# Weight sums and activation differences of the second MLP product: from GpSimd to VectorE

## The chip, the cores and the metric

The kernel runs on one core of a Trainium2 chip. The metric is the device time of one execution in microseconds (us), the median of several. Besides TensorE (matrix products; PE in the profile, and PEld for its loads of the stationary operand) the core has VectorE (DVE), ScalarE (ACT), GpSimd (POOL), and SyncE (SP), whose queue starts the transfers from and to memory. Each engine takes its instructions strictly in the order of its own queue.

## The reference

One layer on 512 positions of width 2048 in float32. A mixing part (RMSNorm, a combined projection, stick-breaking attention, a spatial gating unit, gates, an output projection) gives `x = x + out`. It is untouched here. The part that matters is the MLP behind it:

```python
h2 = rms_norm(x, g_ff[l])
x = x + jnp.square(jax.nn.relu(h2 @ w_ff1[l])) @ w_ff2[l]     # w_ff1: 2048 x 8192, w_ff2: 8192 x 2048
```

## The kernel before

**Two halves of every operand.** TensorE is used with a 32-bit type of reduced precision (float32r), so every operand is split into a high half and a low half that together hold the float32 value. One product is three matmuls: high by high (line 68), and the two mixed ones (lines 69 and 70), in `mm3`. ScalarE makes the high half of a weight tile (`w_hi`, lines 90 and 103), then VectorE the low half (`w_lo = raw - w_hi`, lines 92 and 104). A low half can only start when its high half is done, and the matmul of line 69 or 70 that uses it waits for it. The pairs of halves of a weight tile rotate through three places, so a new high half waits until TensorE is through with the tile three before it.

**The MLP loop.** It runs over 16 blocks f of 512 hidden units (`chunks`). In each, `hidden` makes the first product of block f+1 in two parts p of 256 units: 4 weight tiles of 128x1024 by 24 matmuls, 96 in all; then `relu` on VectorE (line 603) and its square on ScalarE (line 604). `strassen` makes the second product of block f, twice (g = 0 and 1, 1024 output columns each). The order on TensorE is: first part of `hidden`, `strassen` g = 0, second part of `hidden`, `strassen` g = 1, so one f has two halves of 96 + 84 = 180 matmuls each.

**Strassen's scheme.** A 2x2 block product takes 7 multiplications instead of 8. Their names in the code, in TensorE's order, are y11, y21, m7, m6, y22, m4 and m5. Each has 12 matmuls (2 position tiles t, 2 tiles k, 3 of `mm3`). On the weight side they take quarters of the matrix or sums of quarters: `plus` (line 165) makes four sums of 128x1024 elements, for m7, m6, y22 and m5, the first only after the low half of y11 has been made from the same buffer. On the activation side `factors` makes four differences of 128x256 elements for each of the two tiles of block f+1 (lines 615 to 618: the `m` tiles), and then splits seven factors (`ys`, 128x256). `factors` for block f+1 falls into the time of `strassen` g = 1 of block f. Every finished product is added to the result tiles by VectorE (line 643, `x`; 16 additions of 128x512 per `strassen`), and these additions also free the accumulators in PSUM that later products need.

**What sets the order.** The tile framework's scheduler sets each engine's queue at build time, from the program's order and its own estimate of durations; nothing is reordered at run time. In the last block (f = 15) there is no `hidden` any more, so the last three `strassen` (g = 1 of block 14, and both of block 15) follow each other directly.

Of the kernel before, what the change touches and what calls it, by code (L numbers as in the profile page):

```python
# [12 lines left out]
ALU = mybir.AluOpType  # L13
# [20 lines left out]
def tile_hybrid_layer(ctx: ExitStack, tc: tile.TileContext, x, g_mix, w_in, g_q, g_k, ln_g, ln_b,  # L34
# [4 lines left out]
    nc = tc.nc  # L39
# [10 lines left out]
    def slot(name, dt=F32, pool=slots):  # L50
        return pool.tile([P, 512], dt, name=name, tag="slot")
# [14 lines left out]
    def mm3(o, lh, rh, start, stop, **kw):  # L66

        nc.tensor.matmul(o, lhsT=lh[0], rhs=rh[0], start=start, stop=False, **kw)  # L68
        nc.tensor.matmul(o, lhsT=lh[0], rhs=rh[1], start=False, stop=False, **kw)  # L69
        nc.tensor.matmul(o, lhsT=lh[1], rhs=rh[0], start=False, stop=stop, **kw)  # L70
# [24 lines left out]
    def split(src, name, scale=None, pool=slots):  # L95

        hi, lo = slot(name + "_hi", F32R, pool), slot(name + "_lo", F32R, pool)
        split_to(hi, lo, src, scale)
        return hi, lo

    def split_to(hi, lo, src, scale=None):
        if scale is None:
            nc.scalar.copy(out=hi, in_=src)  # L103
            nc.vector.tensor_tensor(out=lo, in0=src, in1=f32(hi), op=ALU.subtract)  # L104
        else:
            nc.scalar.activation(out=hi, in_=src, func=AF.Copy, scale=scale)
            nc.vector.scalar_tensor_tensor(out=lo, in0=src, scalar=scale, in1=f32(hi),
                                           op0=ALU.mult, op1=ALU.subtract)
# [31 lines left out]
    def strassen(wap, r0, c0, lhs, evac):  # L140

        KH = 2

        def piece(name):
            return wpool.tile([P, KH, W], F32R, name=name, tag="w_piece", bufs=6)

        def whole(name):
            return state["whole"].tile([P, KH, W], F32, name=name, tag="whole")

        def quarter(h, c):
            raw = whole("w_raw")
            state["load"] = nc.sync.dma_start(
                out=raw, in_=wap[r0:r0 + 2 * KH * P, c0 + c * W:c0 + (c + 1) * W]
                .rearrange("(k h p) c -> h p k c", p=P, h=2)[h])
            return raw

        w11, w12, w21, w22 = quarter(0, 0), quarter(1, 0), quarter(0, 1), quarter(1, 1)
        sc = whole("w_sum")

        def plus(o, a, b):
            nc.gpsimd.tensor_tensor(out=o, in0=a, in1=b, op=ALU.add)  # L165


        made = {"m7": lambda: plus(w11, w11, w21), "m6": lambda: plus(sc, w11, w22),
                "y22": lambda: plus(w12, sc, w12), "m5": lambda: plus(w21, w21, w22)}
        take = {"y11": w11, "y21": w12, "m7": w11, "m6": sc, "y22": w12, "m4": w22, "m5": w21}  # L170
        banks = {}
        for name, b, first, last in (("y11", 0, True, False), ("y21", 1, True, True),
                                     ("m7", 2, True, False), ("m6", 0, False, False),
                                     ("y22", 1, True, True), ("m4", 2, False, True),
                                     ("m5", 0, False, True)):
            if name in made:
                made[name]()
            hi, lo = piece("w_hi"), piece("w_lo")
            split_to(hi, lo, take[name])
            if first:  # L180
                banks[b] = [(aux if b == 1 else acc)("q") for _ in range(2)]
            for t in range(2):
                o = banks[b][t]
                for k in range(KH):
                    y = [part[:, t * P:(t + 1) * P] for part in lhs(k, name)]
                    mm3(o, y, (hi[:, k, :], lo[:, k, :]), first and k == 0, k == KH - 1,
                        skip_group_check=True)
                evac(name, t, o)
# [210 lines left out]
    for half in range(2):  # L399
# [4 lines left out]
                 lambda tb, o, v=v: v.append(split(o, "v", rstd[:, tb:tb + 1])), "v")  # L404
# [205 lines left out]
    def factors(act):  # L610

        y11, y12, y21, y22 = act[0][:, :HS], act[0][:, HS:], act[1][:, :HS], act[1][:, HS:]
        ta, tb = slot("m"), slot("m")
        m7, m6, m4, m5 = ta[:, :HS], ta[:, HS:], tb[:, :HS], tb[:, HS:]
        nc.gpsimd.tensor_tensor(out=m7, in0=y12, in1=y22, op=ALU.subtract)
        nc.gpsimd.tensor_tensor(out=m6, in0=m7, in1=y11, op=ALU.subtract)
        nc.gpsimd.tensor_tensor(out=m4, in0=y21, in1=m6, op=ALU.add)
        nc.gpsimd.tensor_tensor(out=m5, in0=y11, in1=y12, op=ALU.subtract)
        y = {}
        for name, src in (("y11", y11), ("y21", y21), ("m7", m7), ("m6", m6), ("y22", y22),  # L620
                          ("m4", m4), ("m5", m5)):
            t = slot("ys", F32R)
            y[name] = (t[:, :HS], t[:, HS:])
            split_to(*y[name], src)
        return y
# [6 lines left out]
    for f in range(chunks):  # L632
        ys = [factors(act) for act in ahead]
        ahead = []
        for g in range(2):

            if f < chunks - 1:
                ahead.append(hidden(f + 1, g))

            def evac_y(name, t, o):  # L640
                for half, c, op in takes[name]:
                    a = x2[2 * half + t, 2 * g + c]
                    nc.vector.tensor_tensor(out=a, in0=a, in1=o, op=op)  # L643
                    if f == chunks - 1 and (name, half, c) in (("m4", 0, 1), ("y21", 0, 0),
                                                              ("m5", 1, 1), ("m5", 1, 0)):
                        tb, j = 2 * half + t, 2 * g + c
                        nc.sync.dma_start(out=out[tb * P:(tb + 1) * P, j * W:(j + 1) * W], in_=a)

            strassen(w_ff2[0], f * PAIRS * 2 * P, g * 2 * W, lambda k, name: ys[k][name], evac_y)
# [25 lines left out]
```

## Time and profile before

| | us |
|---|---|
| time, median of 3 runs (2574.0 to 2575.1) | 2575.06 |
| time of the profiled execution | 2574.17 |
| its span, first to last instruction | 2572.5 |
| busy: TensorE / VectorE / ScalarE / GpSimd | 2532.1 / 1438.7 / 852.9 / 589.0 |
| start of the first addition of a second product (line 643) | 1286.5 |

The MLP's second product lies in the second half of the span. Matmuls overlap each other: one of 512 columns is shown with 0.39 us, but the next one starts 0.227 us after it. So the distance between starts is what counts for TensorE, and the same is true, to a smaller degree, for VectorE.

### The profile page before, as it was taken

What the parts mean: (1) busy time and instruction counts of PE and PEld (TensorE: products, weight loads), DVE (VectorE), ACT (ScalarE), POOL (GpSimd) and SP (SyncE); (2) the same over time, 40 slices, a digit from 0 to 9 for tenths busy, and PEclk for the clock granted to TensorE, in tenths of its full rate; (3) what the DMA queues carried; (4) which work ended last, traced back from release to release, by engine and by line L of the source; (5) the groups of instructions that cost most, each with busy time, mean ns of one, the idle gap of its engine ahead of it and who ended that gap; (6) DMA issues with size and microseconds to landing.
All of it is one profiled execution on the core that took longest, in us unless ns stands there. A gap on an engine that the chain in (4) does not pass through costs nothing.

```text
span 2572.5 us, 28610 instructions
## 1 busy us (share of the span) xinstructions
PE 2532.1 (98%) x11306; PEld 2082.1 (81%) x11306; DVE 1438.7 (56%) x1806; ACT 852.9 (33%) x1172; POOL 589.0 (23%) x379
## 2 busy tenths in 40 slices
PE   8999999999999999999999999999999999999998
PEld 7888888888888888888878777887778777877786
DVE  4555563333335333333475767667666767576759
ACT  5333342222223222223333333333332334233333
POOL 0211110000211000100223242414342333324244
PEclk9999999999999999999999999999999999999999
DMA  5332323333332333434233323233323333332323
GB/s 172 90 91 74 90 64 99 93 97 98 115 115 78 99 101 93 129 107 133 88 110 95 115 87 111 89 115 97 101 90 107 102 95 99 98 115 82 114 68 121
DMA packets 169574, 259.83 MB, mean 101 GB/s; under 512 B 8368, under 2 KB 77024, under 8 KB 169440
## 3 DMA queue, kind: packets, MB, share of 16 engines
q1 hardware_dynamic: 169440, 258.01, 32.7%
q8 instruction: 89, 1.46, 0.2%
q14 instruction: 45, 0.37, 0.0%
HBM read 253.78 MB, written 4.19 MB: 100 GB/s over the span
## 4 chain that ended last, share of the span: by engine, by line
PE 87%; DVE 10%; issue 1%; ACT 1%; DMA 0%; POOL 0%; SPq 0%; DVEq 0%; ACTq 0%; POOLq 0%
PE f L69 9%; PE f L68 9%; PE f L70 9%; PE q L69 6%; PE q L70 6%; PE q L68 6%; DVE w_lo L104 4%; DVE ys L104 3%; DVE x L643 3%; PE xo L70 2%; PE xo L69 2%; PE xo L68 2%; PE gb L68 2%; PE gb L70 2%; PE gb L69 2%; PE ga L68 2%
## 5 line engine op out<-in xcount | busy, mean ns | idle before, releaser
L92 DVE TENSOR_TENSOR w_lo<-w_raw,w_hi 128x1024 fp32r<-128x1024 f32 x336 | 414.2, 1233 | 686.5 <-ACT w_hi L90 677.7
L90 ACT CAST w_hi<-w_raw 128x1024 fp32r<-128x1024 f32 x336 | 353.7, 1053 | 988.8 <-PE q L69 190.0
L104 DVE TENSOR_TENSOR w_lo<-w_raw,w_hi 128x1024 fp32r<-128x1024 f32 x192 | 281.9, 1469 | 255.8 <-ACT w_hi L103 255.8
L68 PE MATMUL f<-h2T_hi,w_hi 128*128 128x512 f32 x1024 | 398.6, 389 | 0.0
L69 PE MATMUL f<-h2T_lo,w_hi 128*128 128x512 f32 x1024 | 398.5, 389 | 0.0
L70 PE MATMUL f<-h2T_hi,w_lo 128*128 128x512 f32 x1024 | 397.9, 391 | 0.0
L69 PE MATMUL q<-w_lo,ys 128*128 128x512 f32 x896 | 352.8, 394 | 26.4 <-DVE w_lo L104 26.3
L165 POOL TENSOR_TENSOR w_raw<-w_raw 128x1024 f32<-128x1024 f32 x64 | 183.1, 2862 | 820.0 <-DVE w_lo L104 820.0
L70 PE MATMUL q<-w_hi,ys 128*128 128x512 f32 x896 | 349.0, 389 | 0.0
L643 DVE TENSOR_TENSOR x<-x,q 128x512 f32<-128x512 f32 x512 | 331.0, 676 | 2.3 <-PE q L70 0.6
L103 ACT CAST w_hi<-w_raw 128x1024 fp32r<-128x1024 f32 x192 | 201.8, 1053 | 391.2 <-PE f L69 290.3
L68 PE MATMUL q<-w_hi,ys 128*128 128x512 f32 x896 | 324.0, 391 | 1.5 <-DVE x L643 1.2
L69 PEld LDWEIGHTS q<-w_lo,ys 128*128 128x128 f32 x896 | 168.1, 188 | 74.1 <-DVE w_lo L104 40.0
L70 PEld LDWEIGHTS f<-h2T_hi,w_lo 128*128 128x128 f32 x1024 | 192.2, 188 | 44.2 <-DVE w_lo L92 4.6
L69 PEld LDWEIGHTS f<-h2T_lo,w_hi 128*128 128x128 f32 x1024 | 192.2, 188 | 40.1
L68 PEld LDWEIGHTS f<-h2T_hi,w_hi 128*128 128x128 f32 x1024 | 192.3, 188 | 39.4
L68 PEld LDWEIGHTS q<-w_hi,ys 128*128 128x128 f32 x896 | 168.1, 188 | 40.3 <-issue 3.5
L70 PEld LDWEIGHTS q<-w_hi,ys 128*128 128x128 f32 x896 | 168.3, 188 | 33.8
L68 PE MATMUL gb<-hT_hi,w_hi 128*128 128x512 f32 x256 | 100.3, 392 | 0.2 <-DVE gb L413 0.2
L68 PE MATMUL xo<-w_hi,mT_hi 128*128 128x512 f32 x256 | 100.5, 393 | 0.0
L68 PE MATMUL ga<-hT_hi,w_hi 128*128 128x512 f32 x256 | 100.4, 392 | 0.0
L69 PE MATMUL ga<-hT_lo,w_hi 128*128 128x512 f32 x256 | 100.0, 391 | 0.0
(199 smaller groups left out, 3919.4 us busy)
## 6 DMA issues: line engine op xcount, KB each, us to landing
w_raw<-in_w_ff_dram SPq DMA_DIRECT2D x256, 512.0 KB, 3.7
w_raw<-in_w_in_dram SPq DMA_DIRECT2D x144, 512.0 KB, 3.7
w_raw<-in_w_out_dram SPq DMA_DIRECT2D x32, 512.0 KB, 3.7
w_raw<-in_w_oa_dram SPq DMA_DIRECT2D x16, 512.0 KB, 3.7
w_raw<-in_w_ob_dram SPq DMA_DIRECT2D x16, 512.0 KB, 3.6
x<-in_x_dram SPq DMA_DIRECT2D x16, 256.0 KB, 5.3
out_dram<-x SPq DMA_DIRECT2D x16, 256.0 KB, 2.2
xq<-in_x_dram SPq DMA_DIRECT2D x12, 256.0 KB, 6.4
```

Of the source, the lines that this page charges most:

```text
L68: nc.tensor.matmul(o, lhsT=lh[0], rhs=rh[0], start=start, stop=False, **kw)
L69: nc.tensor.matmul(o, lhsT=lh[0], rhs=rh[1], start=False, stop=False, **kw)
L70: nc.tensor.matmul(o, lhsT=lh[1], rhs=rh[0], start=False, stop=stop, **kw)
L90: nc.scalar.copy(out=hi, in_=raw)
L92: nc.vector.tensor_tensor(out=lo, in0=raw, in1=f32(hi), op=ALU.subtract)
L103: nc.scalar.copy(out=hi, in_=src)
L104: nc.vector.tensor_tensor(out=lo, in0=src, in1=f32(hi), op=ALU.subtract)
L165: nc.gpsimd.tensor_tensor(out=o, in0=a, in1=b, op=ALU.add)
L643: nc.vector.tensor_tensor(out=a, in0=a, in1=o, op=op)
```

## The change

In `strassen` the four weight sums, and in `factors` the four differences, are issued to VectorE instead of GpSimd. Nothing else is written differently. These are 32 times 4 sums of 128x1024 and 32 times 4 differences of 128x256.

```diff
         def plus(o, a, b):
-            nc.gpsimd.tensor_tensor(out=o, in0=a, in1=b, op=ALU.add)
+            nc.vector.tensor_tensor(out=o, in0=a, in1=b, op=ALU.add)
...
-        nc.gpsimd.tensor_tensor(out=m7, in0=y12, in1=y22, op=ALU.subtract)
-        nc.gpsimd.tensor_tensor(out=m6, in0=m7, in1=y11, op=ALU.subtract)
-        nc.gpsimd.tensor_tensor(out=m4, in0=y21, in1=m6, op=ALU.add)
-        nc.gpsimd.tensor_tensor(out=m5, in0=y11, in1=y12, op=ALU.subtract)
+        nc.vector.tensor_tensor(out=m7, in0=y12, in1=y22, op=ALU.subtract)
+        nc.vector.tensor_tensor(out=m6, in0=m7, in1=y11, op=ALU.subtract)
+        nc.vector.tensor_tensor(out=m4, in0=y21, in1=m6, op=ALU.add)
+        nc.vector.tensor_tensor(out=m5, in0=y11, in1=y12, op=ALU.subtract)
```

The scheduler puts the moved instructions into VectorE's queue, so its order is new from the first `factors` on. The first place is the end of a second part of `hidden` and the begin of `strassen` g = 1. VectorE's queue before, from the low half of the last `hidden` tiles (L92) over those of y11 and y21 (L104 x2) to that of m6 (from `w_sum`):

```order
L92 TENSOR_TENSOR w_lo<-w_raw,w_hi 128x1024 x2
L104 TENSOR_TENSOR w_lo<-w_raw,w_hi 128x1024 x2
L603 SCALAR_TENSOR_TENSOR relu<-f_9228,rstd_b 128x512
L603 SCALAR_TENSOR_TENSOR relu<-f_9229,rstd_b 128x512
L104 TENSOR_TENSOR w_lo<-w_raw,w_hi 128x1024
L643 TENSOR_TENSOR x_7982<-x_7982,q 128x512
L643 TENSOR_TENSOR x_7984<-x_7984,q 128x512
L104 TENSOR_TENSOR w_lo<-w_sum,w_hi 128x1024
```

The four sums now stand ahead of the two `relu`. Three follow the low half of y11, one that of y21:

```order
L104 TENSOR_TENSOR w_lo<-w_raw,w_hi 128x1024
L165 TENSOR_TENSOR w_raw<-w_raw 128x1024
L165 TENSOR_TENSOR w_sum<-w_raw 128x1024
L165 TENSOR_TENSOR w_raw<-w_raw 128x1024
L104 TENSOR_TENSOR w_lo<-w_raw,w_hi 128x1024
L165 TENSOR_TENSOR w_raw<-w_sum,w_raw 128x1024
L603 SCALAR_TENSOR_TENSOR relu<-f_9228,rstd_b 128x512
L603 SCALAR_TENSOR_TENSOR relu<-f_9229,rstd_b 128x512
```

Behind the second `relu` the low half of m7 and two additions are now mixed with four differences, up to the low half of m6:

```order
L615 TENSOR_TENSOR m<-relu 128x256
L618 TENSOR_TENSOR m<-relu 128x256
L104 TENSOR_TENSOR w_lo<-w_raw,w_hi 128x1024
L616 TENSOR_TENSOR m<-m,relu 128x256
L643 TENSOR_TENSOR x_7982<-x_7982,q 128x512
L643 TENSOR_TENSOR x_7984<-x_7984,q 128x512
L617 TENSOR_TENSOR m<-relu,m 128x256
L104 TENSOR_TENSOR w_lo<-w_sum,w_hi 128x1024
```

So the low half of m6 has four small instructions more ahead of it. The second place follows directly: VectorE's queue from there to the low half of y22, its last row, before:

```order
L104 TENSOR_TENSOR ys<-relu,ys 128x256
L643 TENSOR_TENSOR x_7982<-x_7982,q 128x512
L104 TENSOR_TENSOR ys<-relu,ys 128x256
L104 TENSOR_TENSOR ys<-m,ys 128x256 x2
L104 TENSOR_TENSOR ys<-relu,ys 128x256
L643 TENSOR_TENSOR x_7984<-x_7984,q 128x512
L104 TENSOR_TENSOR ys<-m,ys 128x256 x2
L104 TENSOR_TENSOR w_lo<-w_raw,w_hi 128x1024
```

And now, with two more differences:

```order
L104 TENSOR_TENSOR ys<-relu,ys 128x256
L643 TENSOR_TENSOR x_7982<-x_7982,q 128x512
L104 TENSOR_TENSOR ys<-relu,ys 128x256
L104 TENSOR_TENSOR ys<-m,ys 128x256 x2
L104 TENSOR_TENSOR ys<-relu,ys 128x256
L643 TENSOR_TENSOR x_7984<-x_7984,q 128x512
L615 TENSOR_TENSOR m<-relu 128x256
L104 TENSOR_TENSOR ys<-m,ys 128x256 x2
L618 TENSOR_TENSOR m<-relu 128x256
L104 TENSOR_TENSOR w_lo<-w_raw,w_hi 128x1024
```

Between the last second `relu` and the low half of y22 there were thus 13 instructions, and there are now 19. In `strassen` g = 0 only the four sums are new, in the same place as above; the rest of its order is as before. In the last block the sums stand among the additions and low halves.

## Rows read from the trace of the kernel before

**Rows 1.** The page, part 1: busy time, share of the span, instructions of each engine.

```profile
PE 2532.1 (98%) x11306; PEld 2082.1 (81%) x11306; DVE 1438.7 (56%) x1806; ACT 852.9 (33%) x1172; POOL 589.0 (23%) x379
```

**Rows 2.** Windows over one f: each engine's busy time (instructions), clock, DMA share.

```profile
1703.68:1744.48 40.80, 40.80 (x181) 33.80 (x180) 25.86 (x29) 12.76 (x13) 10.50 (x5) 1.00 0.34 103
1744.48:1787.71 43.23, 41.71 (x181) 33.55 (x180) 32.12 (x43) 17.15 (x27) 18.86 (x13) 1.00 0.32 98
```

**Rows 3.** Waits from 1280 us on: engine, line, releaser; total us, times, longest.

```profile
PEld q L69 <- DVE w_lo L104: 40.0, 36, 2.1
PE q L69 <- DVE w_lo L104: 26.3, 34, 1.8
...
PEld f L70 <- DVE w_lo L92: 4.6, 14, 0.3
```

**Rows 4.** Timeline of PE: start, us, engine, line, operation, out<-in [idle before <-releaser].

```profile
1336.73 0.50 PE L69 MATMUL q<-w_lo,ys 128*128 128x512 f32 x1 [0.96 <-DVE w_lo L104]
...
1744.48 0.39 PE L68 MATMUL q<-w_hi,ys 128*128 128x512 f32 x1
1744.71 0.39 PE L69 MATMUL q<-w_lo,ys 128*128 128x512 f32 x1
...
1755.36 0.61 PE L68 MATMUL q<-w_hi,ys 128*128 128x512 f32 x2
1756.92 0.50 PE L69 MATMUL q<-w_lo,ys 128*128 128x512 f32 x1 [0.94 <-DVE w_lo L104]
1757.26 0.40 PE L70 MATMUL q<-w_hi,ys 128*128 128x512 f32 x1
...
1760.86 0.50 PE L69 MATMUL q<-w_lo,ys 128*128 128x512 f32 x1 [0.58 <-DVE w_lo L104]
...
1766.26 0.50 PE L70 MATMUL f<-h2T_hi,w_lo 128*128 128x512 f32 x1
...
2433.16 0.50 PE L69 MATMUL q<-w_lo,ys 128*128 128x512 f32 x1 [0.58 <-DVE w_lo L104]
```

**Rows 5.** Timeline of PEld, the weight load of the matmul that starts at 1744.71.

```profile
1744.49 0.19 PEld L69 LDWEIGHTS q<-w_lo,ys 128*128 128x128 f32 x1
```

**Rows 6.** Timeline of DVE around the second half of one f.

```profile
1740.10 1.82 DVE L104 TENSOR_TENSOR w_lo<-w_raw,w_hi 128x1024 fp32r<-128x1024 f32 x1 [4.22 <-ACT w_hi L103]
...
1744.68 0.69 DVE L603 SCALAR_TENSOR_TENSOR relu<-f,rstd_b 128x512 f32<-128x512 f32 x1 [2.03 <-PE f L70]
1745.60 2.03 DVE L104 TENSOR_TENSOR w_lo<-w_raw,w_hi 128x1024 fp32r<-128x1024 f32 x1 [0.23 <-ACT w_hi L103]
1747.55 1.27 DVE L643 TENSOR_TENSOR x<-x,q 128x512 f32<-128x512 f32 x2
...
1749.93 0.95 DVE L104 TENSOR_TENSOR ys<-relu,ys 128x256 fp32r<-128x256 f32 x1
...
1755.66 1.21 DVE L104 TENSOR_TENSOR w_lo<-w_raw,w_hi 128x1024 fp32r<-128x1024 f32 x1
1756.79 0.68 DVE L643 TENSOR_TENSOR x<-x,q 128x512 f32<-128x512 f32 x1
1757.39 0.41 DVE L104 TENSOR_TENSOR ys<-relu,ys 128x256 fp32r<-128x256 f32 x1
1757.72 0.68 DVE L643 TENSOR_TENSOR x<-x,q 128x512 f32<-128x512 f32 x1
```

**Rows 7.** Timeline of POOL in the same stretch.

```profile
1744.15 2.40 POOL L165 TENSOR_TENSOR w_raw<-w_sum,w_raw 128x1024 f32<-128x1024 f32 x1
...
1748.89 1.72 POOL L616 TENSOR_TENSOR m<-m,relu 128x256 f32<-128x256 f32 x1
```

**Rows 8.** Timeline of ACT in the same stretch.

```profile
1752.15 1.05 ACT L103 CAST w_hi<-w_raw 128x1024 fp32r<-128x1024 f32 x1
```

**Rows 9.** Timeline of PE, first matmul of the last three second-product groups.

```profile
2500.82 0.39 PE L68 MATMUL q<-w_hi,ys 128*128 128x512 f32 x1
```

**Rows 10.** Timeline of DVE, its last four instructions.

```profile
2566.51 2.48 DVE L643 TENSOR_TENSOR x<-x,q 128x512 f32<-128x512 f32 x4 [0.65 <-PE q L70]
```

## The prediction

> **What bounds the kernel now.** I read the page first: TensorE is busy for 2532.1 of 2572.5 us [rows 1], so at most some 40 us can be won unless its work shrinks, and it doesn't. The reader is to see there that GpSimd's 23% and VectorE's 56% are means that say nothing of a stretch. The windows came next: one f of the MLP loop has two halves of 180 matmuls each, and at the same granted clock (1.00) the half that ends in `strassen` g = 0 takes 40.80 us and the one that begins with g = 1 takes 43.23 us [rows 2]. 40.80 / 180 is 0.2267 us from matmul to matmul, with nothing lost; so the other half loses 2.43 us. The waits say to whom: low halves of weights (`w_lo`) made by VectorE, 34 times on TensorE itself, 36 on its weight loads, and 14 times a small wait of 0.3 us for a low half of `hidden` [rows 3]. The timeline gives the places [rows 4], for a g = 1 that starts at 1744.48 (call it T). The low half of y22 comes late: line 70's matmul is at 1757.26, where two line 68 and one line 69 behind 1755.36 would put it at 1756.04, so 1.22 us. That of m4 comes late at 1760.86 (0.94 us), and that of the first `hidden` tile at 1766.26 (the rest, 0.27 us). The pair of waits stands in every f from the row at 1336.73 to the one at 2433.16, 14 times; the other 6 of the 34 lie behind them, in the last three `strassen`.
>
> Why is VectorE late there? Its timeline has a low half of 2.03 us and a `ys` of 0.95 us, where the same shapes take 1.21 and 0.41 us ten us later [rows 6]. The long ones lie under GpSimd's sum of 2.40 us from 1744.15 and its difference from 1748.89 on [rows 7]; with GpSimd silent they are short. Additions from PSUM stay at about 0.67 us.
>
> **The change part by part.** VectorE's own prices go by distances between starts in undisturbed rows [rows 6]: a low half 1.13 us (1755.66 to 1756.79), an addition 0.60 (to 1757.39), an instruction of 256 columns 0.33 to 0.34 (to 1757.72), and `relu` 0.62 (0.69 less the same overlap of 0.07). The weight sum on VectorE has no row. Its nearest is the low half, the same operation on the same shape: 1.13 us. The other bound is 2.03, the same under GpSimd's load; I take 1.13, since nothing is left on GpSimd in this stage. A difference goes like `ys`, 0.335 us, upper bound 0.95.
>
> *The four sums.* They move into VectorE's idle time before a `strassen`: it stood idle for 4.22 us before the low half of y21 at 1740.10 [rows 6]. Three sums are 3.4 us and fit. The fourth follows that low half, which falls from 1.82 to 1.21 us, and ends near 1742.6; `relu` comes a few tenths later than now, but TensorE needs the bank that it frees only at the third product (T + 5.4). Cover for the sums is thus the `hidden` part ahead; where there is none (the end of the kernel), they cost. Nothing else stands on GpSimd in this stage, so leaving it wins nothing of itself.
>
> *The differences and the low half of y22.* From the second `relu` at 1744.68 to that low half at 1755.66 VectorE now needs 10.98 us for `relu`, 2 low halves, 4 additions and 7 `ys`: undisturbed that is 0.62 + 2.26 + 2.40 + 2.35 = 7.6 us. So GpSimd's presence costs 3.3 us there, waits of 0.2 us included. The change takes this away and adds six differences, 2.0 us. The low half then starts 1.3 us earlier, at 1754.3 (T + 9.8), and ends at T + 11.0. ScalarE's high half is no hindrance: even now it is done at 1753.2 [rows 8]. TensorE's line 69 matmul is due at T + 11.33 and its weight load 0.22 us ahead [rows 4, 5], at T + 11.11. So it is just in time, with 0.1 us to spare.
>
> *What is late next.* The low half of m4 follows after 1.13 + 1.20 us and ends at T + 13.3 (needed at 13.8); that of m5 two additions and a difference later, T + 16.0 (17.0); that of the first `hidden` tile T + 18.7 (19.3). The seven `ys` of the second tile now stand behind it, where there is room: VectorE has caught up by about T + 27, and then idles. All fit, so the 2.43 us go, but for a reserve: the margin at y22 is thinner than my prices are sure. I leave 0.1 us there. 14 x (2.43 - 0.1) = 32.6 us won; 34.0 if nothing is left.
>
> *The end.* From the first matmul of the last g = 1 of block 14 (2500.82, [rows 9]) no idle stretch is left. VectorE's last four additions start 65.7 us later [rows 10]. Its own work up to them, counted in its new queue from the second `relu` (T + 0.2) on: 48 additions (28.8 us), 19 low halves (21.5), 14 `ys` and 8 differences (7.4), 8 sums (9.0), `relu` (0.6), less the four last additions (2.4): 64.9, so not before T + 65.1. Now each sum of the last two `strassen` also stands ahead of a high half and a low half that TensorE waits for. So the end wins at most 0.6 us, and it loses at most the 11.7 us of its sums and differences (9.0 + 2.7). Waits of this kind are in the rows of the end already, and the relief from GpSimd offsets most of the sums: I take +0.8 us.
>
> The sum against the profiled execution: 2574.17 - 32.6 + 0.8 = 2542.4 us. The median of the runs lies 0.9 us above it, so 2575.06 - 31.8 = **2543 us**, 1.2% less. Everything ahead of the first `factors` has the same queues and stays.
>
> **The rivals.**
> *No overlap on VectorE.* If each new or old instruction in this queue took its full duration, the 20 from `relu` to the low half of y22 would need 0.07 us more each, 1.4 us, and some 1.2 us of the stall would stay; at the end some 95 instructions add 6.6 us. 2543.3 + 14 x 1.1 + 6.6 = 2565 us. Against it: the addition at 1756.79 starts 0.08 us before the end of the low half ahead of it (1755.66 + 1.21) [rows 6]. For it: no row shows an instruction that waits for a result of VectorE itself, as some differences and sums do. [...]
>
> *VectorE is full (slower).* If the long instructions of VectorE are not GpSimd's doing but that of their buffers or of ScalarE's writes beside them, the 3.3 us stay and the 2.0 us of differences come on top, each time, before the low half of y22: 14 x 2.0 = 28 us, and 11.7 us at the end. 2575.06 + 39.7 = 2615 us. The point from which it decides: less than 2.0 of the 3.3 us relieved makes it slower. For it: VectorE is the engine that TensorE waits for, and it gets more work. Against it: the long rows match GpSimd's in time, and long and short ones stand side by side on the same kinds of tile.
>
> *Relief and load cancel.* About 2.0 of the 3.3 us relieved, the end within a few us: 2575 us. It needs just that size, and nothing in the rows points to it. That the change doesn't do what it says is not among the cases: VectorE's new queue holds the instructions.
>
> **How the numbers follow.** The forecast (2537 to 2553) 0.78: its low end is all 34.0 us and a few us at the end, whose low halves TensorE may meet better than I walked it; its high end is 0.4 us left in each f and 5 us lost at the end. No overlap 0.10, cancel 0.04, slower 0.08. The measurement tells 0.2% (5 us) from no change, so faster 0.88, same 0.04, slower 0.08. The range reaches into the first rival: 2536 to 2564 us.
>
> **What would show it.** Right: both halves of an f take the same time, 40.8 to 41.0 us; the waits for `w_lo` of line 104 fall from 34 to about 6, all at the end; low halves stand at 1.21 us and `ys` at 0.41 everywhere in the MLP; sums stand at 1.2 us in what was idle time ahead of y21. The step on y22 is wrong if TensorE still waits there, by the same amount in each f; the step on the sums is wrong if the wait shows at m7 or y21 instead. The price of the end is read from the last addition: 65.7 us behind the first matmul of the last g = 1 before, 66.5 expected. The forecast falls if low halves and `ys` under no GpSimd work still come at 2.0 and 0.95 us, or if a new wait (of ScalarE or of TensorE on an addition) stands where the low half was.

## The result: 2539.85 us, and the profile after

The changed kernel takes 2539.85 us (median of 4 runs, 2539.3 to 2540.5); the kernel before, run beside it, took 2574.53 us (2573.5 to 2575.1). The ratio is 0.9866, its 95% interval 0.9849 to 0.9883: 34.7 us or 1.3% less. The span of the profiled execution fell from 2572.5 to 2538.6 us.

The page of the changed kernel, part 1, to be read against [rows 1]:

```profile
PE 2520.2 (99%) x11306; PEld 2086.5 (82%) x11306; DVE 1550.1 (61%) x2062; ACT 851.6 (34%) x1172; POOL 118.6 (5%) x123
```

GpSimd went from 589.0 to 118.6 us, VectorE from 1438.7 to 1550.1 us. VectorE took over 128 sums of 1.22 us and 128 differences of 0.42 us, 210 us in all, but its busy time rose by only 111 us. Its low halves and `ys` became 82 us shorter in sum at the same time; the rest is that busy time counts the overlap of neighbouring instructions once (0.07 to 0.09 us where they follow directly, as at 1733.51 + 1.22 against 1734.64 below). TensorE's 12 us less are no work saved: in the half with the stalls it was shown busy for 41.71 us [rows 2] with the same matmuls that now take 40.80, 14 times 0.9 us.

The windows of one f of the changed kernel answer to [rows 2], with the same columns:

```profile
1691.23:1732.04 40.81, 40.81 (x182) 33.80 (x181) 29.58 (x33) 12.76 (x13) 0.00 (x0) 1.00 0.34 103
1732.04:1772.84 40.80, 40.80 (x182) 33.80 (x181) 35.72 (x55) 17.06 (x27) 0.00 (x0) 1.00 0.34 104
```

Both halves now take 40.8 us, and so do all 29 half-to-half distances of the loop (40.80). Before, 14 of them were 43.22 to 43.28 us. GpSimd stands still in both.

The waits of the changed kernel from 1280 us on answer to [rows 3]:

```profile
PE q L68 <- ACT w_hi L103: 4.2, 2, 2.6
...
PE q L69 <- DVE w_lo L104: 1.5, 4, 0.6
```

Four waits for `w_lo` of line 104 are left of 34, all behind 2480 us, and the one for `hidden`'s low half is gone. New, but small, are two waits for high halves (2.6 and 1.5 us); they stand in the end as well.

The timeline of VectorE in the changed kernel, for the half that begins with the matmul at 1732.04 (T), answers to [rows 6]:

```profile
1722.21 1.22 DVE L104 TENSOR_TENSOR w_lo<-w_raw,w_hi 128x1024 fp32r<-128x1024 f32 x1 [4.21 <-ACT w_hi L103]
1723.47 1.23 DVE L165 TENSOR_TENSOR w_raw<-w_raw 128x1024 f32<-128x1024 f32 x1
1724.73 1.23 DVE L165 TENSOR_TENSOR w_sum<-w_raw 128x1024 f32<-128x1024 f32 x1
1725.88 1.22 DVE L165 TENSOR_TENSOR w_raw<-w_raw 128x1024 f32<-128x1024 f32 x1
1727.65 1.23 DVE L104 TENSOR_TENSOR w_lo<-w_raw,w_hi 128x1024 fp32r<-128x1024 f32 x1 [0.56 <-ACT w_hi L103]
1728.91 1.22 DVE L165 TENSOR_TENSOR w_raw<-w_sum,w_raw 128x1024 f32<-128x1024 f32 x1
...
1732.23 0.69 DVE L603 SCALAR_TENSOR_TENSOR relu<-f,rstd_b 128x512 f32<-128x512 f32 x1 [1.49 <-PE f L70]
...
1733.51 1.22 DVE L104 TENSOR_TENSOR w_lo<-w_raw,w_hi 128x1024 fp32r<-128x1024 f32 x1
1734.64 0.42 DVE L616 TENSOR_TENSOR m<-m,relu 128x256 f32<-128x256 f32 x1
...
1737.65 0.42 DVE L104 TENSOR_TENSOR ys<-relu,ys 128x256 fp32r<-128x256 f32 x1
...
1741.86 1.22 DVE L104 TENSOR_TENSOR w_lo<-w_raw,w_hi 128x1024 fp32r<-128x1024 f32 x1
...
1744.19 1.22 DVE L104 TENSOR_TENSOR w_lo<-w_raw,w_hi 128x1024 fp32r<-128x1024 f32 x1
...
1746.86 1.22 DVE L104 TENSOR_TENSOR w_lo<-w_raw,w_hi 128x1024 fp32r<-128x1024 f32 x1
...
1749.53 1.22 DVE L92 TENSOR_TENSOR w_lo<-w_raw,w_hi 128x1024 fp32r<-128x1024 f32 x1
```

The reader is to see four things. The sums of line 165 take 1.22 to 1.23 us and stand where VectorE was idle. The low half behind the second `relu` (1733.51) takes 1.22 us, where it took 2.03. The first `ys` (1737.65) takes 0.42 us, where it took 0.95. And the low half of y22 starts at 1741.86 and ends at 1743.08, T + 11.04. TensorE's line 69 matmul that takes it follows without a gap, as the window shows: 40.80 us of 40.80 busy.

### The profile page after: what moved, and what is told of

Its sections match the earlier page's. It is cut to its first block, busy times and chain, and to the rows that moved or that the text cites. A ratio compares the mean times of both kernels' runs of the same rounds, so it can differ in the third digit from the quotient of the medians.

```text
span 2538.6 us, 28443 instructions
## 1 busy us (share of the span) xinstructions
PE 2520.2 (99%) x11306; PEld 2086.5 (82%) x11306; DVE 1550.1 (61%) x2062; ACT 851.6 (34%) x1172; POOL 118.6 (5%) x123
## 4 chain that ended last, share of the span: by engine, by line
PE 96%; DVE 2%; issue 1%; DMA 0%; ACT 0%; POOL 0%; SPq 0%; DVEq 0%; POOLq 0%
PE f L70 9%; PE f L68 9%; PE f L69 9%; PE q L69 9%; PE q L68 9%; PE q L70 9%; PE xo L70 2%; PE xo L69 2%; PE xo L68 2%; PE gb L68 2%; PE gb L70 2%; PE gb L69 2%; PE ga L68 2%; PE ga L69 2%; PE ga L70 2%; PE v L70 1%
## 5 line engine op out<-in xcount | busy, mean ns | idle before, releaser
L92 DVE TENSOR_TENSOR w_lo<-w_raw,w_hi 128x1024 fp32r<-128x1024 f32 x336 | 413.6, 1234 | 672.6 <-ACT w_hi L90 663.8
L643 DVE TENSOR_TENSOR x<-x,q 128x512 f32<-128x512 f32 x512 | 336.8, 683 | 3.5 <-PE q L70 0.6
L104 DVE TENSOR_TENSOR w_lo<-w_raw,w_hi 128x1024 fp32r<-128x1024 f32 x192 | 234.9, 1224 | 133.5 <-ACT w_hi L103 133.5
L70 PE MATMUL ga<-hT_hi,w_lo 128*128 128x512 f32 x256 | 99.9, 392 | 0.0
```

The source lines that it names most:

```text
L92: nc.vector.tensor_tensor(out=lo, in0=raw, in1=f32(hi), op=ALU.subtract)
```

## The experiments

All times below are medians of 4 runs, each compared with runs of the kernel before on the same chip (2573.8 to 2574.2 us). Diffs are against the changed kernel. T is in each the first matmul of `strassen` g = 1 in the same f; the length of its half is the distance from T to the next half's begin.

### Only the sums on VectorE, and only the differences

```diff
 # only the sums: the four differences go back, of which the first is shown
-        nc.vector.tensor_tensor(out=m7, in0=y12, in1=y22, op=ALU.subtract)
+        nc.gpsimd.tensor_tensor(out=m7, in0=y12, in1=y22, op=ALU.subtract)
...
 # only the differences: the sums go back
-            nc.vector.tensor_tensor(out=o, in0=a, in1=b, op=ALU.add)
+            nc.gpsimd.tensor_tensor(out=o, in0=a, in1=b, op=ALU.add)
```

Expected of the sums alone: 

> Only the four weight sums are on VectorE; the four differences stay on GpSimd. Theory A (VectorE was slow because GpSimd's instructions ran beside it, each of them delaying a VectorE instruction with two operands in SBUF): of the 3.3 us by which VectorE was late before the low half of y22, the low half of 2.03 us under the sum is 0.9, and the rest, 2.4 us, lies under the differences and stays. VectorE then needs 7.6 + 2.4 = 10.0 us behind the second relu, the low half of y22 ends at about T + 11.4 against T + 11.1, and 0.3 us of stall stays there, with some of the 0.94 us at m4: 0.5 to 1.2 us for each f, 7 to 17 us in 14 of them. Expected 2552 us (2546 to 2560). Theory B (TensorE waited because the differences themselves came late from GpSimd): moving the sums alone gives little, the stall stays near 2.4 us for each f, 2565 to 2575 us. Theory S (it was the sums alone): all is won, 2540 us.

Measured: 2549.35 us, ratio 0.9905 (0.9889 to 0.9922). The half takes 41.54 to 41.60 us, so 0.74 to 0.80 us are lost in each f, where 2.43 were before. The timeline of VectorE in this run, T = 1735.37:

```profile
1735.57 0.69 DVE L603 SCALAR_TENSOR_TENSOR relu<-f,rstd_b 128x512 f32<-128x512 f32 x1 [1.49 <-PE f L70]
1736.49 1.22 DVE L104 TENSOR_TENSOR w_lo<-w_raw,w_hi 128x1024 fp32r<-128x1024 f32 x1 [0.23 <-ACT w_hi L103]
...
1740.83 1.43 DVE L104 TENSOR_TENSOR w_lo<-w_sum,w_hi 128x1024 fp32r<-128x1024 f32 x1
1742.19 0.95 DVE L104 TENSOR_TENSOR ys<-relu,ys 128x256 fp32r<-128x256 f32 x1
...
1744.88 1.21 DVE L104 TENSOR_TENSOR w_lo<-w_raw,w_hi 128x1024 fp32r<-128x1024 f32 x1
...
1748.21 1.22 DVE L104 TENSOR_TENSOR w_lo<-w_raw,w_hi 128x1024 fp32r<-128x1024 f32 x1
```

The timeline of GpSimd in the same run:

```profile
1741.13 1.73 POOL L618 TENSOR_TENSOR m<-relu 128x256 f32<-128x256 f32 x1
```

The timeline of TensorE in the same run, its wait for the low half of m5:

```profile
1753.16 0.50 PE L69 MATMUL q<-w_lo,ys 128*128 128x512 f32 x1 [0.18 <-DVE w_lo L104]
```

The low half behind `relu` is short again (1.22 us), and those instructions that lie under the differences of line 615 to 618 are long: the low half of m6 takes 1.43 us, and a `ys` 0.95, as does the next one. From `relu` to the low half of y22 VectorE needs 9.31 us instead of 10.98, so moving the sums alone takes away 1.7 of the 3.3 us (I had put 0.9). Not all of this lay under the sums: the differences, too, cost less than before, since in this queue they begin 3 us later and meet other instructions. The low half of y22 ends in time (T + 10.7). What is late is that of m4 and that of m5 (the row at 1748.21, and one at 1751.88), by 0.17 and 0.46 us (the distances of TensorE's matmuls there, less 0.227 for each), since more `ys` stand ahead of them in this queue; the last 0.1 us goes to the some twenty matmuls behind the two waits, many of which are 0.23 to 0.24 us apart. So the size came as theory A had it and the place did not; theories B and S are out by 16 and 9 us.

Expected of the differences alone: 

> Only the four differences are on VectorE; the four weight sums stay on GpSimd. Theory A (GpSimd's instructions delay VectorE's with two operands in SBUF): the differences' 2.4 us of delay go, the 0.9 us under the fourth sum stays (a low half of about 2.0 us for m7), and VectorE has six differences more, 2.0 us: the low half of y22 starts 7.6 + 0.9 + 2.0 = 10.5 us behind the second relu and ends at about T + 11.9, 0.8 us late in each f, 14 times 11 us. Expected 2551 us (2545 to 2560). Theory B (the differences came late from GpSimd): nearly all is won, 2540 to 2543 us. Theory S (the sums alone): nothing is won, or 2.0 us for each f are lost, 2574 to 2602 us.

Measured: 2556.33 us, ratio 0.9933 (0.9918 to 0.9948); the half takes 41.82 to 41.86 us, 1.02 lost. The timeline of VectorE, T = 1736.11:

```profile
1736.31 0.69 DVE L603 SCALAR_TENSOR_TENSOR relu<-f,rstd_b 128x512 f32<-128x512 f32 x1 [2.03 <-PE f L70]
1736.91 1.54 DVE L615 TENSOR_TENSOR m<-relu 128x256 f32<-128x256 f32 x1
...
1747.05 1.22 DVE L104 TENSOR_TENSOR w_lo<-w_raw,w_hi 128x1024 fp32r<-128x1024 f32 x1
```

The timeline of GpSimd in the same run:

```profile
1735.76 2.40 POOL L165 TENSOR_TENSOR w_raw<-w_sum,w_raw 128x1024 f32<-128x1024 f32 x1
```

The timeline of TensorE in the same run:

```profile
1748.33 0.50 PE L69 MATMUL q<-w_lo,ys 128*128 128x512 f32 x1 [0.73 <-DVE w_lo L104]
```

The first difference on VectorE takes 1.54 us where others take 0.42: it waits until GpSimd's sum is over (1735.76 + 2.40 = 1738.16). This 1.13 us puts the low half of y22 at T + 10.94, its end at T + 12.16, and TensorE waits there. Theory A gave 0.8 us in each f; it is 1.0. 14 times 1.02 is 14.3 us, and the span is 15.2 us longer than that of the changed kernel. I had looked for GpSimd's delay in the low half of m7, which now stands two rows later.

Neither part alone gives what both give: theory B (late differences) would have had the whole gain in the second, theory S in the first.

### GpSimd beside VectorE with nobody waiting for it

Three kernels leave the changed kernel's queues on TensorE, VectorE, ScalarE and SyncE exactly as they are and add work on GpSimd at the place of the differences. In this kernel all tiles lie in SBUF but TensorE's accumulators, which lie in PSUM.

```diff
...
+        for a, b in ((y12, m7), (y11, m6), (y21, m4), (y11, m5)):          # reads two
+            nc.gpsimd.tensor_tensor(out=idle, in0=a, in1=b, op=ALU.subtract)
...
+            nc.gpsimd.tensor_copy(out=idle, in_=b)                          # reads one
...
+        nc.gpsimd.tensor_tensor(out=idle[:, :1], in0=y12[:, :1], in1=m7[:, :1], op=ALU.subtract)
+        for _ in range(12):
+            nc.gpsimd.memset(idle, 0.0)                                     # writes
```

Expected of the reads of two operands: 

> The changed kernel with four differences of 128x256 on GpSimd besides, for each of the two tiles, whose result nobody uses; they read a relu tile and an m tile. No engine waits for a result of GpSimd, and the other queues are those of the changed kernel. Theory A (GpSimd's reading delays VectorE's instructions with two operands in SBUF, by about 0.55 us for each of its instructions, as a ys of 0.95 us against 0.41 before): four or five of them fall ahead of the low half of y22, 2.2 to 2.75 us against a margin of 0.1, so TensorE stalls 2.1 to 2.7 us in each f again, and rows of ys and w_lo are long again. Expected 2574 us (2568 to 2580). Theory B (TensorE waited for late results of GpSimd): nothing changes, 2540 us. [...]

Measured: 2559.01 us, ratio 0.9944 (0.9929 to 0.9958); 19.2 us slower than the changed kernel, though nobody waits for GpSimd. The half takes 41.79 to 41.83 us in 11 of the 14 f and 42.3 to 42.4 in three, in sum 15.6 us more. The end is 4.8 us longer; VectorE is full there, so the same delays should count, but I did not take this stretch apart. The timeline of VectorE, T = 1737.20:

```profile
1738.67 1.76 DVE L104 TENSOR_TENSOR w_lo<-w_raw,w_hi 128x1024 fp32r<-128x1024 f32 x1
...
1740.69 1.27 DVE L645 TENSOR_TENSOR x<-x,q 128x512 f32<-128x512 f32 x2
...
1743.36 0.96 DVE L104 TENSOR_TENSOR ys<-relu,ys 128x256 fp32r<-128x256 f32 x1
...
1749.25 1.28 DVE L645 TENSOR_TENSOR x<-x,q 128x512 f32<-128x512 f32 x2
```

The timeline of GpSimd in the same run:

```profile
1738.59 0.76 POOL L620 TENSOR_TENSOR idle<-relu,m 128x256 f32<-128x256 f32 x1 [61.32 <-DVE m L615]
...
1740.92 0.74 POOL L620 TENSOR_TENSOR idle<-relu,m 128x256 f32<-128x256 f32 x1 [1.56 <-DVE m L616]
1742.47 2.44 POOL L620 TENSOR_TENSOR idle<-relu,m 128x256 f32<-128x256 f32 x2 [0.81 <-ACT ys L103]
...
1747.36 2.57 POOL L620 TENSOR_TENSOR idle<-relu,m 128x256 f32<-128x256 f32 x1 [2.44 <-DVE m L615]
```

The timeline of TensorE in the same run:

```profile
1749.39 0.50 PE L69 MATMUL q<-w_lo,ys 128*128 128x512 f32 x1 [0.69 <-DVE w_lo L104]
```

So GpSimd's work alone, with nobody waiting for its results, brings back the long rows and the stall. GpSimd's difference begins at 1738.59; the low half that follows at 1738.67 takes 1.76 us instead of 1.22. The `ys` at 1743.36 takes 0.96 instead of 0.42. Together 1.09 us, and the half is 0.99 us longer: the difference, 0.1 us, is the margin at y22. In the three longer ones a third instruction is hit ahead of it (a pair of `ys` of 1.29 us instead of 0.76), and 1.62 less 0.1 is the 1.5 us lost there. My number was too high (2.2 to 2.75 us of delay, 2574 us), because I had each GpSimd instruction meet a VectorE one. The one at 1740.92 meets the additions from PSUM at 1740.69, which keep their 1.27 us for two. And GpSimd itself waits: the instruction at 1747.36 is shown with 2.57 us, though others take 0.74; it gets through only when VectorE turns to the additions at 1749.25.

Expected of the copies: 

> As the run with GpSimd's unused differences, but each is a copy of 128x256 on GpSimd (one operand read in SBUF, one written) of an m tile. If any read of SBUF by GpSimd delays VectorE's instructions with two operands there, low halves of 1.5 us and more and ys of 0.7 us and more stand under the copies again, and TensorE waits at y22 by the sum of the two delays less 0.1 us: 2550 to 2560 us, depending on how long a copy takes. If it takes two operands on GpSimd's side as well, nothing changes: 2540 to 2542 us.

Measured: 2546.38 us, ratio 0.9893 (0.9878 to 0.9907). The timeline of VectorE, T = 1733.34:

```profile
1734.81 1.42 DVE L104 TENSOR_TENSOR w_lo<-w_raw,w_hi 128x1024 fp32r<-128x1024 f32 x1
...
1739.16 0.62 DVE L104 TENSOR_TENSOR ys<-relu,ys 128x256 fp32r<-128x256 f32 x1
```

The timeline of GpSimd in the same run:

```profile
1734.69 0.46 POOL L620 COPY idle<-m 128x256 f32<-128x256 f32 x1 [62.76 <-DVE m L615]
```

A copy takes 0.46 us, and the two delays are 0.20 us each (1.42 against 1.22, 0.62 against 0.42). 0.40 less the margin of 0.1 is 0.3; the halves take 41.11 to 41.17 us, 0.31 to 0.37 more. One operand read on GpSimd's side was enough here. The time is below the 2550 us that I gave as the lower end, since the delay is the rest of a copy, shorter than I had reckoned.

Expected of the writes: 

> The changed kernel with GpSimd filling a tile of 128x256 with zeros besides, 12 times for each of the two tiles of differences, behind one tiny difference of 128x1 that sets the time; nobody uses the result, and the other queues are those of the changed kernel. So GpSimd only writes. Theory A in its narrow form (it is GpSimd's reads of SBUF that delay VectorE): VectorE's low halves stay at 1.21 us and its ys at 0.41, and the time stays, 2540 us (2538 to 2543). Theory C (any work of GpSimd in SBUF delays VectorE): long rows and stalls at y22 come back, 2550 us or more. [...]

Measured: 2541.98 us, ratio 0.9875 (0.986 to 0.989). The timeline of VectorE, T = 1732.06:

```profile
1733.53 1.22 DVE L104 TENSOR_TENSOR w_lo<-w_raw,w_hi 128x1024 fp32r<-128x1024 f32 x1
```

The timeline of GpSimd in the same run:

```profile
1733.72 4.39 POOL L621 MEMSET idle<- 128x256 f32 x12
```

And the window of the half in the same run:

```profile
1732.06:1772.86 40.80, 40.80 (x182) 33.78 (x180) 35.70 (x55) 17.10 (x27) 9.73 (x26) 1.00 0.33 104
```

GpSimd fills its tile twelve times in 4.39 us right under a low half, and this takes its 1.22 us; all halves take 40.80 us. Theory C is out: these writes didn't delay VectorE. The 2.1 us by which the time is longer don't come from the loop. The spans differ by 1.2 us, all behind its last half, and 1.0 of these stand behind the start of VectorE's last four additions (66.4 us behind the first matmul of the last g = 1, against 66.2), where GpSimd has nothing left to do.

### The margin at the low half of y22

```diff
...
+        nc.vector.tensor_tensor(out=idle, in0=y12, in1=m5, op=ALU.subtract)
+        nc.vector.tensor_tensor(out=idle, in0=y21, in1=m5, op=ALU.subtract)
```

Expected: 

> The changed kernel with two more differences of 128x256 on VectorE for each tile of differences (result used by nobody); two of them stand in VectorE's queue between the second relu and the low half of y22. If the margin there is 0.1 us, as the prediction worked out and as the run with GpSimd's reads suggests (1.09 us of delay, 0.98 us of stall in each f), 2 x 0.335 = 0.67 us more leave a stall of 0.56 to 0.6 us in each f, 14 times 8 us, at that place and nowhere else; at the end of the kernel 1.3 us more. Expected 2549 us (2546 to 2552). Rival: the low half of y22 had more room than 0.3 us, and the stall is under 0.4 us: 2540 to 2546 us.

Measured: 2550.05 us, ratio 0.9908 (0.9893 to 0.9923). The half takes 41.37 us in all 14. The timeline of VectorE, T = 1734.65:

```profile
1745.15 1.22 DVE L104 TENSOR_TENSOR w_lo<-w_raw,w_hi 128x1024 fp32r<-128x1024 f32 x1
```

The low half starts at T + 10.50 instead of T + 9.82, 0.68 us later, and 0.57 us are lost: the margin is 0.11 us. The end is 1.7 us longer (1.3 expected). Three independent delays (1.09, 0.68, 0.40 us) gave 0.99, 0.57 and 0.31 us of stall. So the changed kernel is just in time there, and what VectorE gets to do besides between the second `relu` and this place costs its length less 0.1 us, 14 times.

### The end

```diff
...
+        eng = nc.gpsimd if last_block else nc.vector      # last_block: f == chunks - 1
         def plus(o, a, b):
-            nc.vector.tensor_tensor(out=o, in0=a, in1=b, op=ALU.add)
+            eng.tensor_tensor(out=o, in0=a, in1=b, op=ALU.add)
```

Expected: 

> The changed kernel, but in the last block alone (both strassen of f = 15) the sums are made by GpSimd again; all else stays on VectorE. From the first matmul of the last g = 1 of block 14 to the end of the span it is 72.2 us in the changed kernel; TensorE's work there is 57.1 us, so at most about 10 us can be won. Theory: in the end VectorE is full (idle for under 2 us up to its last four additions), and sums that stand in its queue ahead of high halves are what TensorE waits for (2.6 and 1.5 us); eight sums less are 9.0 us of VectorE's time, of which GpSimd's reads give back some 0.5 to 1 us for each sum. 67 to 71 us from that matmul to the end, 2535 to 2539 us. Rival: the delays by GpSimd take back all of it, 72 us or more, 2540 us or more.

Measured: 2541.54 us, ratio 0.9874 (0.9857 to 0.989); from the first matmul of the last g = 1 of block 14 to the end of the span it is 74.1 us, against 72.2 in the changed kernel. My theory fell, the rival held; this rests on the traces, since the intervals of the two ratios overlap. The timeline of VectorE in the last block:

```profile
2487.82 2.45 DVE L104 TENSOR_TENSOR w_lo<-w_raw,w_hi 128x1024 fp32r<-128x1024 f32 x1
2490.19 5.10 DVE L104 TENSOR_TENSOR ys<-m,ys 128x256 fp32r<-128x256 f32 x2
...
2495.21 3.66 DVE L645 TENSOR_TENSOR x<-x,q 128x512 f32<-128x512 f32 x6
```

The timeline of GpSimd in the same run:

```profile
2489.26 3.25 POOL L167 TENSOR_TENSOR w_sum<-w_raw 128x1024 f32<-128x1024 f32 x1
2492.48 2.53 POOL L167 TENSOR_TENSOR w_raw<-w_raw 128x1024 f32<-128x1024 f32 x1
```

The low half at 2487.82 takes 2.45 us instead of 1.22. Two `ys`, 0.75 us of work, take 5.10 us: each waits for one of GpSimd's sums, which follow each other directly. Six additions that free banks in PSUM stand behind them (2495.21), and TensorE waits for two of these. Its waits from 2466 us on in this run (total us, times, longest):

```profile
PE q L68 <- DVE x L645: 4.8, 2, 3.4
```

I had counted 0.5 to 1 us for each sum; with the sums back to back each of the two `ys` lost 2.2 us ((5.10 - 0.75) / 2), nearly a whole one.

The differences of the last block alone, put back to GpSimd:

```diff
...
-        ys = [factors(act) for act in ahead]
+        ys = [factors(act, nc.gpsimd if f == chunks - 1 else nc.vector) for act in ahead]
```

Expected: 

> The changed kernel, but the eight differences of the last block's activations alone are made by GpSimd again; all sums and the other differences stay on VectorE. From the first matmul of the last g = 1 of block 14 to the end of the span it was 70.7 us in the run with the sums alone on VectorE, which has the same division of work there, and 72.2 us in the changed kernel. Theory: VectorE is full in the end, and 2.7 us of differences less are worth more there than the delay by GpSimd's reads; the halves of all f stay at 40.8 us, the end falls to 70.7 us, and the time by 1.5 us to 2538.4 us, if anything just below what can be measured. Rival: as with the sums of the last block, the delays take it back: 72 us or more, 2540 us or more.

Measured: 2538.99 us (2538.7 to 2539.2), ratio 0.9864 (0.9847 to 0.988), the end 71.3 us, between the theory's 70.7 and the rival's 72. That is 0.9 us less than the changed kernel, whose ratio is 0.9866 with the same width of interval: no difference that these runs can tell. I found no version that is measurably better than the changed kernel.

## Why the prediction was right

**What bounds the kernel** held: 2.43 us in every second half were all there was to win, and all of it was won. 14 x 2.43 = 34.0 us, against a span that is 33.9 us shorter. (One word of it is wrong: the half of 40.80 us begins with g = 0, it doesn't end in it.) The profiled execution was forecast at 2542.4 us and took 2540.31. Of these 2.1 us, 1.4 are the reserve of 0.1 us in each f, which was not needed, and 0.3 the end; the rest is small differences in the loop and ahead of it. The 3.15 us by which 2543 lay too high hold, besides, that the median of the runs now lies 0.5 us below the profiled execution, where I had added 0.9.

**The four sums** stand where the prediction put them, three ahead of the low half of y21 and one behind it, in time that was idle. Their price was a little too low: three of the four start 1.26 us behind the instruction ahead, not 1.13. The second reads the first one's result (1723.47 to 1724.73), and the first and the fourth overwrite the buffer that the low half just ahead of them reads (1722.21 to 1723.47, 1727.65 to 1728.91). The third depends on nothing just ahead and starts 1.15 us behind. As this time was idle, the 0.3 us cost nothing.

**The differences and the low half of y22** came out to the tenth: from `relu` to that low half 9.63 us (7.6 + 2.0 predicted), end at T + 11.04 (T + 11.0), margin 0.1 by the three delays (0.1). TensorE's weight load there starts at T + 11.11, as worked out, some 0.06 us behind that end. This was less than the prices were sure, as the prediction says: that the full 34.0 us were won and not 32.6 was luck, the mechanism was not. So the prices by distance between starts were right, and GpSimd's reading was what had made the rows long: the runs with unused differences and copies bring them back, the run with writes alone does not, and the two runs with one part alone show that it takes both parts.

**What is late next**: nothing, as predicted. Low halves of m4, m5 and the first `hidden` tile end at T + 13.37, 16.04 and 18.71 (13.3, 16.0, 18.7).

**The end** cost 0.5 us instead of 0.8 (72.2 us from the first matmul of the last g = 1 to the end of the span, 71.7 before): the last four additions start 66.2 us behind that matmul (66.5 predicted, 65.7 before). The timeline of VectorE in the changed kernel, its last four additions, and then TensorE's first matmul of that stretch, answering to [rows 9, 10]:

```profile
2532.64 2.48 DVE L643 TENSOR_TENSOR x<-x,q 128x512 f32<-128x512 f32 x4 [0.65 <-PE q L70]
```

The timeline of TensorE in the same run:

```profile
2466.43 0.39 PE L68 MATMUL q<-w_hi,ys 128*128 128x512 f32 x1
```

**The rivals.** No overlap on VectorE: out, its instructions still start up to 0.09 us ahead of the shown end of the one before (1733.51 + 1.22 against the next at 1734.64), and even the dependent sums lose only 0.1 us. With the full shown duration for each instruction, as this rival had it, some 1.2 us would have been lost in each f; no run shows it. VectorE full: out, and so is the partial relief; the condition that it named, long rows that are not GpSimd's doing, is contradicted by the changed kernel, where the same buffers and ScalarE's same work leave a low half at 1.22 us, and by the run with GpSimd's unused differences, where one takes 1.76 us again.

## What to carry to other kernels

Read an engine's instructions at one shape in two places: if the same shape takes 1.2 us here and 2.0 there, look for what another engine does at that moment before looking at the queue. Here moving work *onto* the engine that TensorE waited for made that engine faster, because its partner's reads of SBUF had cost it more (3.3 us) than the moved work (2.0 us). Where a chain ends only 0.1 us ahead of its deadline, work out the margin and say so: here 0.68 us added there cost 0.57 in each f.

## What the hardware showed beside that

In these runs GpSimd and VectorE delayed each other when VectorE's instruction had two operands in SBUF and GpSimd's read there. VectorE's additions with one operand in PSUM kept their length (1.27 us for two), and so did a low half of 1.22 us beside GpSimd's writes. The price was the rest of the instruction that came first (0.54 us for a GpSimd difference of 0.74 us, 0.20 for a copy of 0.46, 1.13 for a sum of 2.40 that was half done: in each case what was left of GpSimd's instruction when VectorE's began, less 0.12 to 0.14), and GpSimd's shown duration held its waits (2.57 us for 0.74 of work).

In the end of the changed kernel TensorE's granted clock falls to 0.50 for 6.8 us (2495.1 to 2501.9), which it didn't do before. Windows of the changed kernel, columns as in [rows 2]:

```profile
2480.00:2499.00 19.00, 13.78 (x54) 9.94 (x53) 19.00 (x30) 4.82 (x6) 0.00 (x0) 0.90 0.15 51
2499.00:2502.00 3.00, 3.00 (x8) 2.32 (x8) 3.00 (x5) 1.04 (x1) 0.00 (x0) 0.51 0.79 191
```

TensorE was busy for 13.78 of 19 us, with its longest waits (2.6 and 1.5 us) at the end of this stretch. In the next 3 us the granted clock is 0.51. The 0.90 of the stretch before is a mean: 0.50 in the last 3.8 us of it and 1.00 ahead. The fall begins some 0.5 us behind the end of the wait of 2.6 us (2494.56); no run shows what causes it. Before, the granted clock was 1.00 in each of the windows of 9 to 10 us from 2500.82 to 2569 us, where TensorE's longest wait for a low half was 1.8 us [rows 3]. Two neighbouring matmuls of that moment:

```profile
2500.05 0.63 PE L69 MATMUL q<-w_lo,ys 128*128 128x512 f32 x1
2500.48 0.63 PE L70 MATMUL q<-w_hi,ys 128*128 128x512 f32 x1
```

They are 0.43 us apart instead of 0.227; over the six distances of this kind that is 1.2 us. Whether this made the end 0.5 us longer is not shown: VectorE is busy for all of both windows, and the run with the last block's differences back on GpSimd has matmuls 0.43 us apart there too (2497.14 to 2500.99), with an end of 71.3 us, shorter than the 71.7 of before.
